# All two-tensor work of GpSimd moved to VectorE, and the gates' last product made a side stream, in a hybrid DeltaNet and pooling block on one core

## The chip, the core and the metric

One core of a Trainium2 chip runs the whole layer. Its engines are TensorE (PE; its weight loads are PEld), VectorE (DVE), ScalarE (ACT), GpSimd (POOL) and SyncE (SP), which issues the transfers. The metric is the device time of one execution in microseconds (us).

## What is computed

One layer of a hybrid block, batch 1: 1024 tokens `x` and 256 context tokens `ctx`, 1024 channels. Normalised and modulated tokens go through one input projection whose columns feed two groups of heads: eight DeltaNet heads (scans in both directions, the tokens' scans starting from the context's final states) and four pooling groups with box means of width 2, 4, 8 and 16. Both are gated by a SiLU, joined, projected, gated, added to `x` and normalised. Cut to what matters:

```python
hn = _rms_norm(h, gain) * (1 + scale) + shift
proj = jnp.einsum('bld,dp->blp', hn, w_in)
qkv, ab, z_dn, u_pool, z_pool = jnp.split(proj, PROJ_SPLITS, axis=-1)
qkv = jax.nn.silu(_short_conv(qkv, conv_w))          # 5 taps
...                                                  # q, k, v per head, l2-normalised
o_f, s_f = _gated_delta_rule(q, k, v, g[0], beta[0], s0_f)
o_b, s_b = _gated_delta_rule(flipped ..., s0_b)
o = _rms_norm(o_f + jnp.flip(o_b, 2), dn_gain) * jax.nn.silu(z_dn)
y_pool = _pool_mixer(u_pool, ...) * jax.nn.silu(z_pool)
y_x = jnp.concatenate([o, y_pool], axis=-1)
out = _rms_norm(x + gate_x * jnp.einsum('blm,md->bld', y_x, w_out), final_gain)
...                                                  # delta rule, a chunk: q_dec = q * exp(g)
v_new = u_i - w_i @ state
o_i = q_dec_i @ state + qk_i @ v_new
state = state * exp(g_last) + k_tail_i^T @ v_new
```

## The kernel before

**Precision.** The input projection is made in a split form. Each weight tile (1024 x 128, `wraw`) is copied to a rounded `whi` on ACT, and the rest, `wlo = wraw - whi`, is made on POOL; the activations have `hnhi` and `hnlo` likewise. Three matmuls per k step (hi by hi, hi by lo, lo by hi) make 24 for a half tile of 512 tokens (rows `mm<-hnhi,whi`, `mm<-hnhi,wlo`, `mm<-hnlo,whi`; in the context's tiles of 256 tokens the sources are called `D` and `zs`). The output projection does the same with `yhi`, `ylo`, `wohi` and `wolo`.

**Stages.** Modulation and the context's tiles (the head of the program, to some 165 us); then for each of the eight heads four projection tiles, v, k, z, q (to 925); then the pooling (to 1110) and the output projection. A head's q, k and v pass a convolution of five taps (`conv_post`): four multiply-adds on VectorE per half, `kT<-u,cw,kT` and its like, a tanh on ACT, and a last product. A gate tile (`gate_tile`: z of the heads, the pooling's u and z) takes a tanh on ACT to `tmp`, and a product on VectorE, `zs<-tmp,mm` or `u<-tmp,mm`.

**The scan.** Beside the projection run side streams: the inverse of each block's triangular matrix (`B`, `bt`, `VV`, `XT`, many small matmuls), the decays `D` (loaded, then masked by selects on POOL), `ks` (scaled keys) and `qd` (queries times their decay, two products of 128x1024 per head on POOL, in `stage_s`), and the scan itself: `sc` and `o` on TensorE, `r` and the state `S` on VectorE. `sm<-sm,expo` on POOL is a power for the norms.

**Order.** The order on each engine is made by a planner while the program is written (class `Flow`). The main stream is the projection, a matmul at a time; a side stream is advanced when its next step is due by the planner's own cost of each instruction (`spend` adds it to the engine). A step that yields a name such as ("conv", i) waits until that flag is set. `conv_tile` waits for the convolution two tiles back, so a k tile waits for the q of the head before: the pause of the main matmuls there is called a seam below. In `spend`, `hold` prices the overlap of POOL's two-tensor work with VectorE's (0 through the heads, 0.9 in the pooling stage).

Of the kernel before, what the change touches and what calls it, by code (L numbers as in the profile page):

```python
# [11 lines left out]
ACTF = mybir.ActivationFunctionType  # L12
ALU = mybir.AluOpType
# [4 lines left out]
P = 128  # L18
# [22 lines left out]
LAG = 6  # L41
T_MOD = 36000.0
T_X = 1500.0
XD = 2
WD = 0
DY = 2
XACT = 9
# [22 lines left out]
class Flow:  # L70
# [3 lines left out]
    def __init__(self):  # L74
        self.free = dict(pe=0.0, act=0.0, dve=0.0, pool=0.0, sync=0.0)
        self.dma = 0.0
        self.cur = None
        self.flags = {}
        self.sides = []
        self.seen = {}, {}  # L80
        self.slots = {}
        self.stored = 0.0
        self.banks = [0.0, 0.0]
        self.port = dict(dve=[], pool=[])

        self.hold = 0.0


    def born(self, name, place, bufs):
# [39 lines left out]
                            del old[r]  # L129
            self.seen[w].setdefault(name, {})[p0, p1, f0, f1, eng] = end  # L130

    def spend(self, eng, ns, uses, shared=False):
        hold = self.hold
        start = self.start(eng, uses)
        end = start + ns
        if shared:

            there = self.port["pool" if eng == "dve" else "dve"]
            both = sum(max(0.0, min(end, b) - max(start, a)) for a, b in there)
            if eng == "dve":  # L140
                end += hold * both
            else:
                self.free["dve"] += hold * both
            self.port[eng] = self.port[eng][-3:] + [(start, end)]
        self.free[eng] = end
        self.note(eng, uses, end)
        t = self.cur
        if t is not None:
            t.next = max(t.next, end + NEXT[eng])
            t.last = eng  # L150
# [177 lines left out]
class Engine:  # L328
# [46 lines left out]
    def __getattr__(self, op):  # L375
        f = getattr(self.real, op)

        def call(*a, **k):
            u = self.uses(op, a, k)
            shared = (op == "tensor_tensor" if self.name == "pool" else  # L380
                      self.name == "dve" and not any(v[0].split("_")[0] in PSUM_TAGS for v in u))
            self.flow.spend(self.name, self.cost(op, a, k), u, shared)
            return f(*a, **k)  # L383

        return call
# [24 lines left out]
def kernel(  # L410
# [235 lines left out]
    def hnc(b, k, t0=0):  # L646
        return (hnc_lo if b else hnc_hi)[k // 4][:, k % 4, :]
# [3 lines left out]
    def ctx_split(k):  # L651
        tp = pp_tile()
        for i, xt in enumerate(cx_t):
            pe.transpose(tp[:, i * P:(i + 1) * P], xt[:, k * P:(k + 1) * P], ident)
        h32 = dl_tile([P, 512], "tmp", 2)
        act.activation(out=h32[:, 0:LC], in_=tp[:, 0:LC], func=ACTF.Identity,
                       scale=md[:, 1, 1, k:k + 1], bias=md[:, 1, 0, k:k + 1])
        dve.tensor_copy(hnc(0, k), h32[:, 0:LC])
        (dve if k % 2 else pool).tensor_tensor(out=hnc(1, k), in0=h32[:, 0:LC], in1=hnc(0, k), op=ALU.subtract)

    def hnx(b, k, t0):
        return hn[2 * (t0 // 512) + b][:, k, :]
# [26 lines left out]
    def split(raw, hi, lo, e):  # L689

        act.activation(out=hi, in_=raw, func=ACTF.Copy)
        e.tensor_tensor(out=lo, in0=raw, in1=hi, op=ALU.subtract)

    def w_split(n, part):
        if n >= len(order):
            return
        if part == 0:
            wq[n] = [gemm.tile([P, KT, P], FP32R, tag=f"w{s}", bufs=2, name=f"w{s}") for s in ("hi", "lo")]
        hi, lo = wq[n]
        s = slice(part * (KT // 2), (part + 1) * (KT // 2))  # L700
        split(raws[n][:, s, :], hi[:, s, :], lo[:, s, :], dve if n < WD and part else pool)

    arrs = [{a: const.tile([P, 16, n], FP32, name=f"{a}{i}") for a in ("ngc", "neg", "edl", "egl", "beta")}
            for i, n in enumerate((NBC, NB))]
# [37 lines left out]
    def gemm_take():  # L742
        i = cur[0]
        cur[0] += 1
        if i + 2 < N2:
            w_load(i + 2)
        return i, wq.pop(i)

    def gemm_half(i, w, src, t0, m, evac):
        ps = mm_tile()  # L750
        j = 0
        for k in range(KT):
            for a, b in PASSES:
                pe.matmul(ps[:, 0:m], w[a][:, k, :], src(b, k, t0),
                          start=(j == 0), stop=(j == 3 * KT - 1))
                j += 1
                if t0 == 0 and j == (4 if i > 1 else 14) and i:
                    w_split(i + 1, 0)
                if t0 == 0 and j == (14 if i > 1 else 18) and i:
                    w_split(i + 1, 1)  # L760
                    if i + 2 >= N2:
                        w_load(i + 2)
                yield
        evac(ps[:, 0:m], t0)

    def gemm_tile(src, n, evac):
        i, w = gemm_take()
        for t0 in range(0, n, 512):
            yield from gemm_half(i, w, src, t0, min(512, n), evac)

# [46 lines left out]
        if name:  # L817
            flow.flag(*name)

    def gate_tile(src, dst, tmp=lambda: dl_tile([P, 512], "tmp", 2)):  # L820
        def evac(ps, t0):
            t = tmp()
            act.activation(out=t, in_=ps, func=ACTF.Tanh, scale=0.5)
            dve.scalar_tensor_tensor(out=dst[:, t0:t0 + 512], in0=t, scalar=1.0, in1=ps,
                                     op0=ALU.add, op1=ALU.mult)

        yield from gemm_tile(src, L, evac)


    ab_src = {}  # L830
# [430 lines left out]
    def stage_s(J):  # L1261

        J.qd = [J.load_rows(escr, d, dl_tile([P, 8 * P], "qd", 2)) for d in range(2)]
        yield from stage_k(J)
        for d in range(2):
            pool.tensor_tensor(out=J.qd[d], in0=J.qd[d], in1=J.qT, op=ALU.mult)
        flow.flag("q", J.key)

    def scan_step(J, blocks, S, Sn, first, last, o, ostart):
# [190 lines left out]

    def z_tile(h):
        zs = dl_tile([P, L], "zs", 2)
        yield from gate_tile(hnx, zs)
        jobs[h].zs = zs
        flow.flag("z", h)

    def zp_tile(t):

        yield ("hn",)
        if t > 1:  # L1470
            yield ("zp", t - 2)
        zs = dl_tile([P, L], "ks", 2)
        yield from gate_tile(hnx, zs)
        sync.dma_start(out=zscr[CH[t]], in_=zs)
        flow.flag("zp", t)

    def zp_late(t):
        i = convs[0]
        yield ("conv", i - 2)
        zs = dl_tile([P, L + 4], "u", 2)  # L1480
        convs[0] += 1
        yield from gate_tile(hnx, zs)
        sync.dma_start(out=zscr[CH[t]], in_=zs[:, 0:L])
        flow.flag("conv", i)

    def u_early(n):

# [126 lines left out]
    for k in range(KT):  # L1614
        if k == PRE:
            for g, n in zip(start, (2, 3, 3)):
                for _ in range(n * KT // 2):
                    next(g)
        mod_part(1, mod_ps[1], k)
        if k < KT // 2:  # L1620
            ctx_split(k)
        if k >= SPOS and k - SPOS < 4:
            w_split((k - SPOS) // 2, (k - SPOS) % 2)
    act.activation(out=alg, in_=alg, func=ACTF.Exp)
    mod_end(1, mod_ps[1])
    for k in range(KT // 2, KT):
# [3 lines left out]
    flow.add(gate_all(), [("k", -1)])  # L1630
    flow.run(main())
    flow.drain()
    flow.hold = 0.9
    dl.release()


# [22 lines left out]
    def icnt_tile(hw):  # L1659
        f = [pl([P, GW], f"ic{i}") for i in range(3)]  # L1660
        r = []
        for n, t in ((GW, f[0]), (GR, f[1])):
            pool.tensor_scalar(out=t[:, 0:n], in0=idf[:, 0:n], scalar1=float(hw), scalar2=float(n),
                               op0=ALU.add, op1=ALU.min)
            pool.tensor_scalar(out=f[2][:, 0:n], in0=idf[:, 0:n], scalar1=float(-hw), scalar2=0.0,
                               op0=ALU.add, op1=ALU.max)
            pool.tensor_tensor(out=t[:, 0:n], in0=t[:, 0:n], in1=f[2][:, 0:n], op=ALU.subtract)
            dve.reciprocal(out=t[:, 0:n], in_=t[:, 0:n])
            r.append(t[:, 0:n])
        ic = pl([P, GR, GW], "icnt", 2)  # L1670
        pool.tensor_tensor(out=ic, in0=rep(r[0], GR), in1=bc(r[1], GW), op=ALU.mult)
        return ic

    def window_ranges(m, n):
# [128 lines left out]
    def u_tiles(between):  # L1803
# [10 lines left out]
        for a in post:  # L1814
            if a == "z":
                t, zs = next(stage)
                yield from gate_tile(hnx, zs, lambda: pl([P, 512], "ws", 3))
                sync.dma_start(out=zscr[t], in_=zs)
                flow.flag("zl", t)
                continue  # L1820
            if n >= NU:
                yield ("up", CH[n - NU])
# [7 lines left out]
            if n < KT - 2:  # L1830
                yield from gemm_tile(hnx, L, evac)
                flow.flag("u", n)
            else:
                last.append((n, *gemm_take(), evac))
                yield from gemm_half(*last[-1][1:3], hnx, 0, 512, evac)
            n += 1
        between()
# [9 lines left out]
    def out_main():  # L1847
# [18 lines left out]
        def load_split(hi, lo, src, eng, name, after=None):  # L1866
# [4 lines left out]
            def thread():  # L1871
# [15 lines left out]
                yield after  # L1887
                if after:
                    yield
                yield eng  # L1890
                h, l = (hi, lo)
                if after:
                    h, l = wo[name[1]] = hi()
                split(r, h, l, dve if eng == "dve" else pool)
                free_raw(slot)
                flow.flag(*name)

# [88 lines left out]

        def second_half():
            yield ("mixed",)
            flow.hold = 0.0
# [113 lines left out]
```

## Time and profile before

| what | value |
|---|---|
| median of 3 runs | 1295.55 us (1290.17 to 1296.2) |
| the profiled execution | 1298.5 us, its span 1296.8 us |
| mean granted TensorE clock | 0.966 |
| busy in the span | PE 1205.6, DVE 906.3, ACT 582.3, POOL 412.7 us |

The times in the rows count from the first instruction of the span. A row of instructions gives how many there were, what they took in all, the mean of one, and behind a second bar how long the engine had been idle just before them and what ended that. L383 is a helper through which each instruction of the kernel before is recorded (L366 in the changed one), so rows are told apart by tile names.

### The profile page before, as it was taken

To read this page: it belongs to the slowest core of one execution; us is meant where nothing else is said; L and a number is where in the kernel's file an instruction comes from. 1 tells how busy PE (TensorE), PEld (TensorE's weight loads), DVE (VectorE), ACT (ScalarE), POOL (GpSimd) and SP (SyncE) were. 2 spreads that over 40 slices of the span, in tenths; PEclk is the share of its full clock that TensorE was granted. 3 is DMA by queue.
4 is the path that set the end of the run, shared out by engine and by line. 5 is a ranking of instruction groups with operands and counts; after the bars stand their busy time and mean duration, and the time that the engine had idled before them with its cause. 6 is when DMAs were issued, how large, how long until landed. Compare 5 with 4: busy or idle time off the path is not lost.

```text
span 1296.8 us, 26417 instructions
## 1 busy us (share of the span) xinstructions
PE 1205.6 (93%) x10631; PEld 968.8 (75%) x10631; DVE 906.3 (70%) x1867; ACT 582.3 (45%) x1514; POOL 412.7 (32%) x447
## 2 busy tenths in 40 slices
PE   7875799999899999999999999999999998989997
PEld 1674677787687877877778778778788886768886
DVE  4798689769785777787887887888434999733212
ACT  2476637543445537555474474653613223222110
POOL 2466433121321423324233142141215643313230
PEclk9898799899898999999999999999999998999999
DMA  9542255222121323112221132122313135574230
GB/s 318 208 114 82 58 144 155 75 58 69 43 62 22 102 50 103 41 43 87 65 86 39 47 102 58 46 80 51 96 58 106 49 122 187 175 251 134 83 113 33
DMA packets 157384, 123.73 MB, mean 95 GB/s; under 512 B 47106, under 2 KB 135115, under 8 KB 157261
## 3 DMA queue, kind: packets, MB, share of 16 engines
q1 hardware_dynamic: 157261, 122.04, 31.3%
q8 instruction: 83, 1.36, 0.4%
q14 instruction: 40, 0.33, 0.1%
HBM read 101.43 MB, written 20.60 MB: 94 GB/s over the span
## 4 chain that ended last, share of the span: by engine, by line
PE 54%; DVE 26%; ACT 8%; DMA 5%; issue 4%; POOL 2%; SPq 0%; DVEq 0%; POOLq 0%; ACTq 0%
PE mm L383 34%; PE sc L383 6%; DVE kT L383 6%; PE o L383 6%; DVE t L383 5%; PE pp L383 5%; PE pa L383 4%; DVE vT L383 3%; ACT junk L383 2%; DVE qT L383 1%; DVE B L383 1%; DVE D L383 1%; ACT u L383 1%; DVE ws L383 1%; ACT ks L383 1%
## 5 line engine op out<-in xcount | busy, mean ns | idle before, releaser
L383 PE MATMUL mm<-hnhi,wlo 128*128 128x512 f32 x768 | 319.0, 415 | 0.0
L383 PE MATMUL mm<-hnhi,whi 128*128 128x512 f32 x768 | 318.7, 415 | 0.0
L383 PE MATMUL mm<-hnlo,whi 128*128 128x512 f32 x768 | 315.7, 411 | 0.0
L383 POOL TENSOR_TENSOR wlo<-wraw,whi 128x512 fp32r<-128x512 f32 x110 | 159.0, 1452 | 389.5 <-ACT whi L383 385.5
L383 PEld LDWEIGHTS mm<-hnhi,wlo 128*128 128x128 f32 x768 | 146.7, 191 | 24.7 <-issue 0.9
L383 PEld LDWEIGHTS mm<-hnhi,whi 128*128 128x128 f32 x768 | 146.8, 191 | 23.8 <-issue 0.9
L383 PEld LDWEIGHTS mm<-hnlo,whi 128*128 128x128 f32 x768 | 146.8, 191 | 22.7
L383 DVE SCALAR_TENSOR_TENSOR kT<-u,cw,kT 128x512 f32<-128x512 f32 (+1 forms) x96 | 99.1, 1035 | 5.4 <-ACT kT L383 1.8
L383 ACT ACTIVATE y<-sc 128x256 f32<-128x256 f32 (+1 forms) x65 | 25.1, 386 | 126.4 <-PE sc L383 121.0
L383 DVE SCALAR_TENSOR_TENSOR t<-t,laneN 128x1 f32<-128x1 f32 (+4 forms) x150 | 62.7, 418 | 13.8 <-POOL t L383 8.2
L383 ACT ACTIVATE u<-mm 128x512 f32<-128x512 f32 (+1 forms) x64 | 34.6, 541 | 80.9 <-PE mm L383 80.9
L383 ACT ACTIVATE whi<-wraw 128x512 fp32r<-128x512 f32 x110 | 67.2, 631 | 2.1 <-DMA wraw<-in_w_in_dram 1.8
L383 DVE SCALAR_TENSOR_TENSOR vT<-u,cw,vT 128x512 f32<-128x512 f32 (+1 forms) x80 | 66.4, 838 | 1.8
L383 DVE TENSOR_TENSOR pw<-mm,zp 128x512 f32<-128x512 f32 (+1 forms) x12 | 8.0, 669 | 81.3 <-PE mm L383 81.3
L383 ACT ACTIVATE D<-D,ngc 128x128 f32<-128x128 f32 x160 | 53.1, 404 | 25.9 <-POOL D L383 25.7
L383 DVE SCALAR_TENSOR_TENSOR qT<-u,cw,qT 128x512 f32<-128x512 f32 (+1 forms) x80 | 61.3, 772 | 3.9 <-ACT qT L383 2.2
L383 DVE SCALAR_TENSOR_TENSOR S<-S,egl,sc 128x128 f32<-128x128 f32 x112 | 33.6, 341 | 35.6 <-PE sc L383 33.1
L383 DVE SCALAR_TENSOR_TENSOR r<-sc,neg,vn 128x128 f32<-128x128 f32 x128 | 38.6, 343 | 16.7 <-PE sc L383 16.7
L383 DVE SCALAR_TENSOR_TENSOR D<-pp,sm,D 128x128 f32<-128x128 f32 x128 | 35.6, 343 | 20.3 <-PE pp L383 20.3
L383 PEld LDWEIGHTS sc<-r,B 128*128 128x128 f32 x256 | 36.1, 190 | 18.1 <-issue 8.2
L383 PE MATMUL sc<-r,B 128*128 128x128 f32 x256 | 40.9, 282 | 9.3 <-DVE r L383 9.3
L383 PE MATMUL sc<-S,kT 128*128 128x128 f32 x256 | 40.8, 282 | 8.8 <-DVE S L383 8.6
(411 smaller groups left out, 2759.8 us busy)
## 6 DMA issues: line engine op xcount, KB each, us to landing
wraw<-in_w_in_dram SPq DMA_DIRECT2D x55, 512.0 KB, 3.9
D<-gscr SPq DMA_DIRECT2D x40, 256.0 KB, 4.0
qd<-escr SPq DMA_DIRECT2D x16, 512.0 KB
kT<-in_w_in_dram SPq DMA_DIRECT2D x9, 512.0 KB, 4.0
whnhi<-in_w_mod_dram SPq DMA_DIRECT2D x8, 512.0 KB, 3.6
whnlo<-in_w_mod_dram SPq DMA_DIRECT2D x8, 512.0 KB, 9.0
D<-in_w_mod_dram SPq DMA_DIRECT2D x8, 512.0 KB, 3.6
yscr<-zs SPq DMA_DIRECT2D x8, 512.0 KB, 2.9
```

Source lines behind the costliest of these rows:

```text
L383: return f(*a, **k)
```

## The change

What POOL did with two tensors goes to VectorE: the weights' low parts, low parts of activations (`XD`, the context's split), the `qd` products, the inverse counts `icnt`, and the low parts of the output projection. POOL keeps the selects, the powers and the memsets. The low part of a weight is now a side stream of its own (`w_low`, put first among the side streams), and `gemm_take` waits for both of its halves. The gate's last product becomes a side stream (`gate_mul`), with the store and the flag behind it, and a half tile waits for the gate product two back. The planner's price of overlap (`hold`, `port`) is gone. In the loading of the output weights the ACT and the VectorE part are separate steps.

```diff
-XD = 2
+XD = 1
...
-    def spend(self, eng, ns, uses, shared=False):
-        hold = self.hold
+    def spend(self, eng, ns, uses):
         start = self.start(eng, uses)
-        end = start + ns
-        if shared:
-
-            there = self.port["pool" if eng == "dve" else "dve"]
-            both = sum(max(0.0, min(end, b) - max(start, a)) for a, b in there)
-            if eng == "dve":
-                end += hold * both
-            else:
-                self.free["dve"] += hold * both
-            self.port[eng] = self.port[eng][-3:] + [(start, end)]
-        self.free[eng] = end
+        end = self.free[eng] = start + ns
...
-        (dve if k % 2 else pool).tensor_tensor(out=hnc(1, k), in0=h32[:, 0:LC], in1=hnc(0, k), op=ALU.subtract)
+        dve.tensor_tensor(out=hnc(1, k), in0=h32[:, 0:LC], in1=hnc(0, k), op=ALU.subtract)
...
-    def w_split(n, part):
+    def w_split(n, part, now=False):
         if n >= len(order):
             return
         if part == 0:
             wq[n] = [gemm.tile([P, KT, P], FP32R, tag=f"w{s}", bufs=2, name=f"w{s}") for s in ("hi", "lo")]
-        hi, lo = wq[n]
-        s = slice(part * (KT // 2), (part + 1) * (KT // 2))
-        split(raws[n][:, s, :], hi[:, s, :], lo[:, s, :], dve if n < WD and part else pool)
+        hi, lo = (t[:, part * (KT // 2):(part + 1) * (KT // 2), :] for t in wq[n])
+        raw = raws[n][:, part * (KT // 2):(part + 1) * (KT // 2), :]
+        act.activation(out=hi, in_=raw, func=ACTF.Copy)
+        flow.flag("whi", n, part)
+        if now:
+            dve.tensor_tensor(out=lo, in0=raw, in1=hi, op=ALU.subtract)
+            flow.flag("wlo", n, part)
+        else:
+            flow.add(w_low(n, part, raw, hi, lo), [("whi", n, part)], True)
+
+    def w_low(n, part, raw, hi, lo):
+        yield "dve"
+        dve.tensor_tensor(out=lo, in0=raw, in1=hi, op=ALU.subtract)
+        flow.flag("wlo", n, part)
+        if part and n + 1 >= N2:
+            w_load(n + 1)
...
     def gemm_take():
         i = cur[0]
         cur[0] += 1
+        for part in range(2):
+            if ("wlo", i, part) not in flow.flags:
+                yield ("wlo", i, part)
         if i + 2 < N2:
             w_load(i + 2)
         return i, wq.pop(i)
 
     def gemm_half(i, w, src, t0, m, evac):
+        if gates[0] and ("gate", gates[0] - 1) not in flow.flags:
+            if ("gate", gates[0] - 2) not in flow.flags and gates[0] > 1:
+                yield ("gate", gates[0] - 2)
...
-                    if i + 2 >= N2:
-                        w_load(i + 2)
...
-        i, w = gemm_take()
+        i, w = yield from gemm_take()
...
+    gates = [0]
+
+    def gate_tile(src, dst, tmp=lambda: dl_tile([P, 512], "tmp", 2), store=None, name=None):
+
         def evac(ps, t0):
+            n = gates[0]
+            gates[0] += 1
             t = tmp()
             act.activation(out=t, in_=ps, func=ACTF.Tanh, scale=0.5)
-            dve.scalar_tensor_tensor(out=dst[:, t0:t0 + 512], in0=t, scalar=1.0, in1=ps,
-                                     op0=ALU.add, op1=ALU.mult)
+            flow.flag("tanh", n)
+            flow.add(gate_mul(n, t, ps, t0, dst, store, name), [("tanh", n)], True)
 
         yield from gemm_tile(src, L, evac)
+
+    def gate_mul(n, t, ps, t0, dst, store, name):
+        yield "dve"
+        dve.scalar_tensor_tensor(out=dst[:, t0:t0 + 512], in0=t, scalar=1.0, in1=ps, op0=ALU.add, op1=ALU.mult)
+        flow.flag("gate", n)
+        if t0:
+            if store is not None:
+                sync.dma_start(out=store, in_=dst[:, 0:L])
+            flow.flag(*name)
...
-            pool.tensor_tensor(out=J.qd[d], in0=J.qd[d], in1=J.qT, op=ALU.mult)
+            yield "dve"
+            dve.tensor_tensor(out=J.qd[d], in0=J.qd[d], in1=J.qT, op=ALU.mult)
...
         zs = dl_tile([P, L], "zs", 2)
-        yield from gate_tile(hnx, zs)
+        yield from gate_tile(hnx, zs, name=("z", h))
         jobs[h].zs = zs
-        flow.flag("z", h)
...
-    flow.hold = 0.9
...
-        pool.tensor_tensor(out=ic, in0=rep(r[0], GR), in1=bc(r[1], GW), op=ALU.mult)
+        dve.tensor_tensor(out=ic, in0=rep(r[0], GR), in1=bc(r[1], GW), op=ALU.mult)
...
-                yield eng
+                yield "act"
                 h, l = (hi, lo)
                 if after:
                     h, l = wo[name[1]] = hi()
-                split(r, h, l, dve if eng == "dve" else pool)
+                act.activation(out=h, in_=r, func=ACTF.Copy)
+                yield
+                yield "dve"
+                dve.tensor_tensor(out=l, in0=r, in1=h, op=ALU.subtract)
```

The planner orders the rest anew. Three places follow.

TensorE, in the head: `mm` are the context's projection tiles, `pp<-ident,...` and `pa` the transposes and products that prepare the blocks of the tokens' scan. Before:

```order
L383 MATMUL mm<-D_220,wlo 128x256
L383 MATMUL pp<-ident,B 128x128 x8
L383 MATMUL pp<-ident,ks 128x128 x2
L383 MATMUL pp<-ident,qd 128x128 x2
L383 MATMUL pa<-kT 128x128 x4
L383 MATMUL pp<-ident,ks 128x128 x2
L383 MATMUL pp<-ident,qd 128x128 x2
L383 MATMUL pp<-kT 128x128 x4
```

and in the changed kernel, where the same step comes some 95 rows sooner:

```order
L366 MATMUL pa<-kT 128x128 x4
L366 MATMUL pp<-ident,ks 128x128 x2
L366 MATMUL pp<-ident,qd 128x128 x2
L366 MATMUL mm<-D_219,whi 128x256
L366 MATMUL mm<-zs,whi 128x256
L366 MATMUL mm<-D_219,wlo 128x256
L366 MATMUL mm<-D_219,whi 128x256
L366 MATMUL mm<-zs,whi 128x256
```

Before, the transposes stand in one piece behind the last of the context's matmuls; now they stand between the context's matmuls, two or three at a time.

VectorE, where a head's k taps run (`kT<-u,cw,kT`). Before:

```order
L383 SCALAR_TENSOR_TENSOR kT<-u,cw,kT 128x512 x4
L383 TENSOR_SCALAR VV<-pp 32x8x32 x2
L383 SCALAR_TENSOR_TENSOR kT<-u,cw,kT 128x512 x4
L383 TENSOR_SCALAR B<-pp 64x8x64
L383 SCALAR_TENSOR_TENSOR zs<-tmp,mm 128x512
L383 SCALAR_TENSOR_TENSOR r<-sc,neg_234,vn 128x128 x2
L383 SCALAR_TENSOR_TENSOR kT<-u,kT 128x512 x2
L383 TENSOR_TENSOR B<-pa,ident 128x512
```

and in the changed kernel:

```order
L366 SCALAR_TENSOR_TENSOR kT<-u,cw,kT 128x512 x2
L366 TENSOR_TENSOR wlo<-wraw,whi 128x512
L366 SCALAR_TENSOR_TENSOR kT<-u,cw,kT 128x512 x2
L366 TENSOR_TENSOR wlo<-wraw,whi 128x512
L366 SCALAR_TENSOR_TENSOR kT<-u,cw,kT 128x512 x4
L366 TENSOR_TENSOR qd<-qd,qT 128x1024 x2
L366 TENSOR_SCALAR B<-pp 64x8x64
L366 SCALAR_TENSOR_TENSOR zs<-tmp,mm 128x512
L366 SCALAR_TENSOR_TENSOR kT<-u,kT 128x512 x2
```

The two weight lows and the pair of `qd` products stand among the taps now, and `r` stands behind the taps' last products.

TensorE, in the seam ahead of head 6's k tile, from the last matmul of the tile before to the first of the k tile. Before:

```order
L383 MATMUL mm<-hnhi_225,wlo 128x512
L383 MATMUL o<-y,D_6622 128x128 x2
L383 MATMUL pa<-laneN,B 32x16 x16
L383 MATMUL sc<-S,kT 128x128 x2
L383 MATMUL pa<-laneN,B 32x16 x16
L383 MATMUL o<-S,qd 128x128 x2
L383 MATMUL pp<-qT,kT 128x128 x4
L383 MATMUL pa<-laneN,bt 32x16 x16
L383 MATMUL sc<-r,B 128x128 x2
L383 MATMUL pa<-laneN,bt 32x16 x16
```

and in the changed kernel:

```order
L366 MATMUL mm<-hnhi_225,wlo 128x512
L366 MATMUL sc<-r,B 128x128 x2
L366 MATMUL pa<-laneN,B 32x16 x16
L366 MATMUL o<-y,D_6581 128x128 x2
L366 MATMUL pa<-laneN,B 32x16 x16
L366 MATMUL pa<-laneN,bt 32x16 x32
L366 MATMUL pa<-t_8420,XT 32x16 x48
L366 MATMUL pp<-qT,kT 128x128 x4
L366 MATMUL pa<-t_8420,XT 32x16 x16
L366 MATMUL pp<-ident,ks 128x128 x4
L366 MATMUL mm<-hnhi_223,whi 128x512
```

The scan's steps are fewer in the seam now; small products `pa<-t,XT` of the inverse and the transposes of `ks` stand in it instead.

## Rows read from the trace of the kernel before

**Rows 1.** The page: busy time, share and instructions of each engine; the chain by engine.
```profile
PE 1205.6 (93%) x10631; PEld 968.8 (75%) x10631; DVE 906.3 (70%) x1867; ACT 582.3 (45%) x1514; POOL 412.7 (32%) x447
...
PE 54%; DVE 26%; ACT 8%; DMA 5%; issue 4%; POOL 2%; SPq 0%; DVEq 0%; POOLq 0%; ACTq 0%
```
**Rows 2.** The span in five windows: length, busy us of each engine, granted clock, DMA.
```profile
0.00:165.00 165.00, 123.72 (x646) 89.48 (x647) 119.78 (x235) 90.47 (x206) 81.23 (x126) 0.86 0.48 156
165.00:500.00 335.00, 320.56 (x3793) 255.92 (x3791) 257.54 (x613) 166.98 (x456) 87.70 (x97) 0.97 0.28 76
500.00:925.00 425.00, 406.50 (x4386) 332.79 (x4386) 338.87 (x796) 230.38 (x675) 121.77 (x124) 1.00 0.23 65
925.00:1110.00 185.00, 179.29 (x1019) 146.75 (x1019) 127.62 (x149) 55.86 (x115) 83.72 (x68) 0.98 0.35 110
1110.00:1297.00 187.00, 175.51 (x795) 143.88 (x793) 62.52 (x77) 38.62 (x63) 38.28 (x32) 0.97 0.41 131
```
**Rows 3.** The same view of one stretch of the head.
```profile
114.60:142.00 27.40, 12.96 (x64) 10.65 (x62) 22.02 (x48) 18.38 (x34) 15.09 (x13) 0.62 0.13 39
```
**Rows 4.** TensorE's waits, 50 to 165: total us, times, longest.
```profile
PE pp L383 <- ACT W L383: 10.7, 2, 9.8
```
**Rows 5.** TensorE's waits, 500 to 925.
```profile
PE sc L383 <- DVE r L383: 9.3, 9, 1.6
PE sc L383 <- DVE S L383: 6.9, 7, 1.6
```
**Rows 6.** Timelines of GpSimd and VectorE from 593: start, us, instruction, count.
```profile
594.99 5.61 POOL L383 TENSOR_TENSOR qd<-qd,qT 128x1024 f32<-128x1024 f32 x2
...
593.07 8.08 DVE L383 SCALAR_TENSOR_TENSOR kT<-u,cw,kT 128x512 f32<-128x512 f32 x4
```
**Rows 7.** Timeline of VectorE at 732.
```profile
732.45 1.54 DVE L383 SCALAR_TENSOR_TENSOR qT<-u,cw,qT 128x512 f32<-128x512 f32 x2
```
**Rows 8.** VectorE's instructions by form: busy us, mean ns | idle before, releaser.
```profile
L383 DVE SCALAR_TENSOR_TENSOR kT<-u,cw,kT 128x512 f32<-128x512 f32 x64 | 77.5, 1215 | 2.6
...
L383 DVE SCALAR_TENSOR_TENSOR qT<-u,cw,qT 128x512 f32<-128x512 f32 x64 | 49.2, 774 | 1.2
...
L383 DVE SCALAR_TENSOR_TENSOR zs<-tmp,mm 128x512 f32<-128x512 f32 x16 | 11.0, 687 | 13.7 <-ACT tmp L383 13.7
...
L383 DVE SCALAR_TENSOR_TENSOR u<-tmp,mm 128x512 f32<-128x512 f32 x12 | 8.2, 686 | 19.9 <-ACT tmp L383 19.9
...
L383 DVE TENSOR_TENSOR hnlo<-XT,hnhi 128x512 fp32r<-128x512 f32 x4 | 2.7, 686 | 2.2 <-ACT hnhi L383 2.2
```
**Rows 9.** GpSimd's instructions by form, whole span.
```profile
L383 POOL TENSOR_TENSOR wlo<-wraw,whi 128x512 fp32r<-128x512 f32 x110 | 159.0, 1452 | 389.5 <-ACT whi L383 385.5 <-issue 3.8
L383 POOL TENSOR_TENSOR qd<-qd,qT 128x1024 f32<-128x1024 f32 x16 | 42.7, 2692 | 0.0
...
L383 POOL TENSOR_TENSOR wlo<-kT,whi 128x512 fp32r<-128x512 f32 x18 | 24.3, 1359 | 9.0 <-ACT whi L383 8.9
```
**Rows 10.** Timeline of VectorE in the pooling stage.
```profile
1008.46 1.23 DVE L383 TENSOR_TENSOR ws<-ws,icnt 128x1024 f32<-128x1024 f32 x1
```
**Rows 11.** VectorE's instructions by form, 50 to 165.
```profile
L383 DVE SCALAR_TENSOR_TENSOR kT<-u,cw,kT 128x256 f32<-128x256 f32 x28 | 19.6, 701 | 2.6 <-ACT kT L383 1.8
L383 DVE SCALAR_TENSOR_TENSOR vT<-u,cw,vT 128x256 f32<-128x256 f32 x16 | 14.8, 925 | 0.5
```
**Rows 12.** Timeline of VectorE at 60.
```profile
60.09 0.48 DVE L383 SCALAR_TENSOR_TENSOR kT<-u,cw,kT 128x256 f32<-128x256 f32 x1
```
**Rows 13.** TensorE's waits, 165 to 500.
```profile
PE o L383 <- DVE qd L383: 3.9, 3, 3.1
```
**Rows 14.** The window view of the seam before head 6's k tile.
```profile
734.10:739.30 5.20, 5.20 (x156) 4.58 (x155) 4.08 (x12) 2.24 (x4) 0.14 (x2) 1.00 0.01 3
```
**Rows 15.** Timelines of ScalarE and GpSimd, 739 to 751.
```profile
740.52 0.28 ACT L383 ACTIVATE junk<-o 128x128 f32<-128x128 f32 x1 [0.68 <-PE o L383]
...
747.84 2.18 ACT L383 ACTIVATE ks<-o,sm 128x128 f32<-128x128 f32 x8
...
745.55 2.26 POOL L383 TENSOR_TENSOR sm<-sm,expo 128x8 f32<-128x8 f32 x1
```

More of the change, by code (lines that the diff above doesn't have):

```diff
@@ L83, in __init__ @@
         self.banks = [0.0, 0.0]
-        self.port = dict(dve=[], pool=[])
-        self.hold = 0.0
     def born(self, name, place, bufs):
@@ L378, in call @@
         def call(*a, **k):
[L379 to L382, printed above, removed]
+            self.flow.spend(self.name, self.cost(op, a, k), self.uses(op, a, k))
             return f(*a, **k)
@@ L818, in conv_post @@
             flow.flag(*name)
-    def gate_tile(src, dst, tmp=lambda: dl_tile([P, 512], "tmp", 2)):
+    gates = [0]
+    def gate_tile(src, dst, tmp=lambda: dl_tile([P, 512], "tmp", 2), store=None, name=None):
         def evac(ps, t0):
+            n = gates[0]
+            gates[0] += 1
             t = tmp()
             act.activation(out=t, in_=ps, func=ACTF.Tanh, scale=0.5)
-            dve.scalar_tensor_tensor(out=dst[:, t0:t0 + 512], in0=t, scalar=1.0, in1=ps,
-                                     op0=ALU.add, op1=ALU.mult)
+            flow.flag("tanh", n)
+            flow.add(gate_mul(n, t, ps, t0, dst, store, name), [("tanh", n)], True)
         yield from gemm_tile(src, L, evac)
+    def gate_mul(n, t, ps, t0, dst, store, name):
[6 more added lines that the diff above has]
+            flow.flag(*name)
     ab_src = {}
@@ L1472, in zp_tile @@
         zs = dl_tile([P, L], "ks", 2)
-        yield from gate_tile(hnx, zs)
-        sync.dma_start(out=zscr[CH[t]], in_=zs)
-        flow.flag("zp", t)
+        yield from gate_tile(hnx, zs, store=zscr[CH[t]], name=("zp", t))
     def zp_late(t):
@@ L1481, in zp_late @@
         convs[0] += 1
-        yield from gate_tile(hnx, zs)
-        sync.dma_start(out=zscr[CH[t]], in_=zs[:, 0:L])
-        flow.flag("conv", i)
+        yield from gate_tile(hnx, zs, store=zscr[CH[t]], name=("conv", i))
     def u_early(n):
@@ L1622 @@
         if k >= SPOS and k - SPOS < 4:
-            w_split((k - SPOS) // 2, (k - SPOS) % 2)
+            w_split((k - SPOS) // 2, (k - SPOS) % 2, True)
     act.activation(out=alg, in_=alg, func=ACTF.Exp)
@@ L1816, in u_tiles @@
                 t, zs = next(stage)
-                yield from gate_tile(hnx, zs, lambda: pl([P, 512], "ws", 3))
-                sync.dma_start(out=zscr[t], in_=zs)
-                flow.flag("zl", t)
+                yield from gate_tile(hnx, zs, lambda: pl([P, 512], "ws", 3), zscr[t], ("zl", t))
                 continue
@@ L1833, in u_tiles @@
             else:
-                last.append((n, *gemm_take(), evac))
+                last.append((n, *(yield from gemm_take()), evac))
                 yield from gemm_half(*last[-1][1:3], hnx, 0, 512, evac)
@@ L1988, in second_half @@
             yield ("mixed",)
-            flow.hold = 0.0
             yield ("pw", GROUPS[-1])
```

## Prediction

> **What bounds the kernel now.** I read the busy shares first, then the chain that ended last, then the span cut into stages, then TensorE's waits in each stage. TensorE (PE) is busy 1205.6 of 1296.8 us, VectorE (DVE) 906.3, GpSimd (POOL) 412.7; the chain runs 54% through PE and 26% through DVE, 2% through POOL [rows 1]. So PE sets the pace and DVE is who it waits for. The stages say where: PE's idle time is 165 - 123.7 = 41 us in the head, 335 - 320.6 = 14 us up to 500, 425 - 406.5 = 18.5 us in the steady heads, 6 us in the pooling stage and 11.5 us in the output projection [rows 2]. PE's work is the same before and after the change (the same matmuls), so the time can only come out of these 91 us, out of the clock, or be added to them.
>
> In the head the largest piece is 114.6 to 142, where PE has 13 us of work in 27.4 at a granted clock of 0.62, which is TensorE's lower level (1.2 GHz) for most of the stretch [rows 3]; one wait of 9.8 us stands in it [rows 4]. The main matmuls of the projection stop there: all that is left of preparing the scan's first blocks stands in the program at that one place. In the steady heads nearly all the named waits are for DVE's `r` and `S`, 9.3 + 6.9 us [rows 5].
>
> **What the change gives DVE back.** While POOL ran a pair of `qd` products (5.61 us), four k taps on DVE took 8.08 us [rows 6]; undisturbed, two taps took 1.54 [rows 7]. So the pair cost DVE 8.08 - 4 x 0.77 = 5.0 us, 0.89 us of DVE for each us of POOL. The means agree: k taps, which lie beside the weights' low parts and `qd`, take 1215 ns, q taps of the same shape 774 [rows 8]. From below, the 64 k taps alone give back 64 x 0.44 = 28 us. From above, POOL's low parts and `qd` in the table (159.0 + 42.7 + 24.3 = 226 us, [rows 9]) times 0.89 would be 201, but much of that lies beside idle DVE or one-input work. A sum over all forms, mean less the shortest instance, gives about 120; I take that.
>
> The Trainium skill ("SBUF — State Buffer", section "Who interferes with whom") states that a DVE instruction with two SBUF inputs and a GpSimd instruction that reads SBUF share a port as an exclusive lock, so that the later one stops until the first is done. The rows of the pair agree nearly fully (0.89 where the lock alone would give at most 1.0, or 5.6 us instead of 5.0). By that rule the selects on `D` that stay on POOL would go on holding DVE up; the sum takes nothing back for these.
>
> **What the change adds to DVE.** 128 low parts of weights (110 + 18 by POOL's rows) at 0.686 us, the time of the same subtraction of that shape on DVE [rows 8]: 88 us. 16 `qd` products of 128x1024 at 1.23 us, an undisturbed product of that shape [rows 10]: 20. Activations' low parts, output lows and inverse counts, some 40 instructions by the same two prices: about 36. Together 144 us. DVE's volume thus goes from 906 to 906 + 144 - 120 = 930 (72%), or, with the lower bound of 28, to 1022 (79%). In volume the change is about neutral; what counts is the place.
>
> **Head.** The order of DVE's instructions before the first `bt<-B` (139.6 us before) holds 30 weight lows, 9 activation lows and 4 context lows more, and 22 taps fewer: 39 x 0.686 + 4 x 0.48 - 22 x 0.48 = 18 us more. Given back: taps of 128x256 take 701 and 925 ns [rows 11] where an undisturbed one takes 0.48 [rows 12]: 28 x 0.22 + 16 x 0.44 = 13 us, with the q taps and tap ends 23, with all two-input forms 33. So DVE comes there 5 to 15 us sooner. PE's stop at 114.6 is a wait for just this work, and in the changed order its transposes stand among the context's matmuls instead of behind them, so PE meets DVE's work without a second bill. A lower bound of nothing isn't excluded: two milestones further on DVE's lead is 7. I take **-11**, above the middle, since the 27.4 us at 0.62 also give clock back.
>
> **165 to 500.** 14 us idle, of which one wait of 3.1 us is for `qd` [rows 13], now made earlier in DVE's own order. The same means speak for a gain: **-3**, bounds 0 and -8.
>
> **500 to 925.** Each head's k taps run into `qd`. Before: 8.08 us for four taps, then `B`, `zs`, `r`. After: 4 x 0.77 + 2 x 1.23 = 5.5, then `B`, `zs`, two more products, `r`: 1.0 us sooner for `r`, and other instructions come 2.6 sooner. I take half of the 16.2 us of `r` and `S` waits: -8, bounds 0 and -16. DVE was at 339 of 425 [rows 2]; new there are 40 lows and 10 `qd`, 27 + 12 = 40 us, and back come 18 (k taps alone) to 37 (all forms): 80 to 85% busy.
>
> Against that stand the seams. A k tile may start only when the convolution of the q two tiles back is finished; before the k tile of head 6 the main matmuls pause from 734.1 to 739.3, 5.2 us, filled with 156 small matmuls [rows 14]. In the changed order three of the eight seams also hold the transposes of `ks`, behind this chain: `o` ready, eight sums of squares on ACT (3.1 us), POOL's power (2.26), four of eight scalings on ACT (1.1) [rows 15]. With the 0.68 us before the first sum and the hops between engines that is some 7.5 us behind the first matmul, a hole of 9 instead of 5.2, of which 2.4 us is PE work that was done elsewhere before: +1.4 each, **+4** for the three. Net **-4**.
>
> **Gates.** The gate's last product stood in the main stream, and DVE waited for ACT's tanh before it, 13.7 + 19.9 us in all [rows 8]. As a side stream it lets other DVE work go first. I cost it at nothing, since DVE isn't the bound in those stretches and PE's next tile covers it (the gate's PSUM bank is asked for two halves later); without that cover a half tile would wait for one product, 0.69 us.
>
> **Pooling and output.** PE idles 6 and 11.5 us there. The lows of `y` and the output weights (13 of 1024 columns and smaller) cost DVE some 30 us where it is 69% busy and 33% busy [rows 2], and about as much contention leaves. **0**, bounds -5 and +6.
>
> **The sum.** -11 - 3 - 4 + 0 = -18. The profiled execution took 1298.5 us (span 1296.8), so 1280.5 on its basis; the median of the runs shown is 1295.55, 3 below, which makes **1278**.
>
> **Rivals.**
> Large gain: the head gives its 15, and the waits between 165 and 925 go almost wholly (25 of 33 us idle), the seams costing nothing. 1295.5 - 40 = 1256. For it: the means of the taps show DVE held up everywhere; against it: DVE isn't emptier, only smoother.
> No change: the head gives 5, the waits halve to no effect since `r` comes only 1.0 us sooner, the seams take 4: 1295.5 - 5 - 3 + 4 = 1291.5, up to 1297. For it: volume is neutral, and four fifths of PE's idle time lie outside the steady heads.
> Slower: the seams decide. If in all eight of them the chain over ACT and POOL ends last and no PE work moves into the hole, each costs 9 - 5.2 = 3.8 us: +30, less the head's 11: 1295.5 + 19 = 1314.5. It decides from three seams' full price (11) upward. What speaks for it is that DVE then has 80 to 85% and every late `qT` makes the next k tile late; against it, that the order shows `ks` in three seams only. The Trainium skill ("Perfetto Trace Analysis", section "Optimizing Scalar/DVE Operations") says that work may be taken off a saturated DVE, to GpSimd even, though the shared port may eat the gain. By its first half this change goes the wrong way, by its second it costs nothing; the row of the pair, 5.0 us of DVE lost for 2.5 us of work moved, bears out the second.
>
> **How the numbers follow.** The forecast has 0.45 (its own range 1266 to 1289), the large gain 0.20, no change 0.19, slower 0.16. Faster, same and slower part at 0.5% of the median, 1289.1 and 1302.0, about what a measurement of this kernel can tell from no change: 0.65, 0.19, 0.16. For 8 in 10 the range must take in most of the large gain and all of no change: 1252 to 1302, leaving out the slower case and 4 in 100 at the low end.
>
> **What would show it.** Right: k taps of 512 columns near 0.77 us; `qd` near 1.23 on DVE; the stretch at 114.6 shorter by about 11 us; `r` and `S` waits near 8 us in the steady heads; DVE near 930 us busy. Wrong: k taps still over 1 us (something else on POOL holds them); seams over 9 us at every k tile; PE waiting for `wlo`, now on DVE behind taps, in the steady heads (each tile's lows are due half a tile ahead, so I expect none); DVE over 1000 us.

## The result, and the profile after

The changed kernel takes 1270.89 us (median of 4 runs, 1267.3 to 1271.24) against 1293.33 before (1290.17 to 1296.2): a ratio of 0.9824, 95% interval 0.9802 to 0.9845, 22 us less. The forecast was 1278, 17.5 less. The profiled execution took 1271.0 us, 27.5 less than the one of before.

The page of the changed kernel, busy times and the chain [rows 1]:

```profile
PE 1199.5 (95%) x10631; PEld 969.3 (76%) x10631; DVE 915.1 (72%) x2050; ACT 579.8 (46%) x1514; POOL 109.0 (9%) x264
...
PE 65%; DVE 14%; issue 8%; ACT 7%; DMA 5%; POOL 0%; SPq 0%; DVEq 0%; POOLq 0%; ACTq 0%
```

GpSimd has lost 304 of its 413 us, and VectorE has gained only 9, with 183 instructions more. What GpSimd keeps is selects, memsets and powers; the powers are products of two tensors too, but small ones (128x8), so the title's "all" goes a little too far. TensorE's idle time fell from 91 to 70 us, its busy time by 6. The instructions of VectorE by form say why its volume stood still [rows 8, 9]:

```profile
L366 DVE TENSOR_TENSOR wlo<-wraw,whi 128x512 fp32r<-128x512 f32 x110 | 75.8, 695 | 11.2 <-ACT whi L366 11.1
L366 DVE SCALAR_TENSOR_TENSOR kT<-u,cw,kT 128x512 f32<-128x512 f32 x64 | 48.2, 760 | 2.0
...
L366 DVE TENSOR_TENSOR qd<-qd,qT 128x1024 f32<-128x1024 f32 x16 | 19.1, 1218 | 0.0
...
L366 DVE SCALAR_TENSOR_TENSOR zs<-tmp,mm 128x512 f32<-128x512 f32 x16 | 11.0, 684 | 2.7 <-ACT tmp L366 2.4
...
L366 DVE SCALAR_TENSOR_TENSOR u<-tmp,mm 128x512 f32<-128x512 f32 x12 | 8.2, 682 | 12.7 <-ACT tmp L366 12.7
```

A k tap takes 760 ns where it took 1215; a weight's low part takes 0.695 us on VectorE where it took 1.45 on GpSimd. Behind the second bar stands the other half: VectorE waited 15 us for the gates' tanh, where it had waited 34.

To compare stages, the windows must end at the same work, not at the same time. The ends chosen are the starts of the projection's main matmuls 480, 1248 and 2208 (counted from 0 in order of time, without those of the modulation) and the last one of the pooling's tiles. Before:

```profile
0.00:181.70 181.70, 140.42 (x964) 99.80 (x965) 131.56 (x254) 96.60 (x220) 87.55 (x131) 0.87 0.50 157
181.70:509.60 327.90, 313.45 (x3549) 253.26 (x3548) 253.43 (x605) 168.84 (x466) 83.55 (x94) 0.97 0.26 71
509.60:934.80 425.20, 406.70 (x4498) 332.36 (x4498) 333.14 (x789) 227.01 (x664) 120.87 (x124) 1.00 0.24 68
934.80:1084.50 149.70, 149.48 (x761) 124.44 (x759) 100.70 (x127) 41.80 (x92) 64.32 (x61) 1.00 0.31 98
1084.50:1296.80 212.30, 195.52 (x866) 158.95 (x864) 87.50 (x95) 48.05 (x74) 56.42 (x39) 0.96 0.42 133
```

and in the changed kernel:

```profile
0.00:160.30 160.30, 135.76 (x963) 94.73 (x964) 123.40 (x308) 97.95 (x226) 21.33 (x81) 0.89 0.57 179
160.30:482.80 322.50, 312.06 (x3622) 252.63 (x3621) 261.99 (x641) 171.49 (x478) 28.95 (x62) 0.98 0.27 76
482.80:915.50 432.70, 412.84 (x4461) 342.03 (x4461) 334.29 (x836) 223.20 (x658) 36.97 (x70) 0.96 0.22 64
915.50:1062.90 147.40, 147.07 (x725) 123.07 (x724) 106.02 (x163) 40.08 (x82) 15.80 (x35) 1.00 0.33 103
1062.90:1269.30 206.40, 191.77 (x867) 156.84 (x865) 89.41 (x105) 47.11 (x71) 5.99 (x16) 0.97 0.42 134
```

The head gained 21.4 us, the first heads 5.4, the pooling 2.3, the output 5.9; the steady heads lost 7.5, and their granted clock fell from 1.00 to 0.96. Of these 7.5 us TensorE is idle for 1.4 more (18.5 before, 19.9 now) and busy for 6.1 more, with 37 matmuls fewer in the stage. The lower clock comes in four stretches of 34 us in all, where the granted clock is 0.50, the lower level (1.2 GHz); three begin inside one of the last seams, while TensorE stands or does small matmuls, and one 4 us behind the seam at 532. In the kernel before no stretch of the steady heads is at that level. One of the four:

```profile
794.10:804.30 10.20, 7.92 (x148) 6.94 (x149) 8.28 (x19) 8.57 (x25) 2.22 (x3) 0.50 0.01 3
```

The stop of the main matmuls [rows 3] is gone: in 106 to 124, where the transposes stand now, TensorE is busy 17.3 of 18 us at full clock.

```profile
106.00:124.00 18.00, 17.31 (x99) 14.60 (x99) 17.55 (x41) 14.19 (x37) 1.27 (x2) 1.00 0.44 119
```

In the steady heads the waits for `r` and `S` [rows 5] have nearly gone, and another has come. TensorE's waits, 500 to 925:

```profile
PE pa L366 <- ACT t L366: 11.5, 4, 3.6
...
PE sc L366 <- DVE r L366: 1.3, 1, 1.3
```

Three of the four, 3.3 to 3.6 us long, stand in the last three seams. Timelines of TensorE and ScalarE at the seam ahead of head 6's k tile [rows 14, 15]:

```profile
709.99 1.48 PE L366 MATMUL pa<-t,XT 32*32 32x16 f32 x96 [3.56 <-ACT t L366]
...
705.54 0.28 ACT L366 ACTIVATE junk<-o 128x128 f32<-128x128 f32 x1 [0.80 <-PE o L366]
...
708.62 1.05 ACT L366 ACTIVATE u<-qT 128x1024 f32<-128x1024 f32 x1
709.56 0.37 ACT L366 ACTIVATE t<-pa 128x256 f32<-128x256 f32 x1
```

ScalarE does the eight sums of squares, then the q tanh, and only then the copy `t` that TensorE needs. The last main matmul before this seam and the first after it start 11.9 us apart, against 5.2 before.

### The profile page after: what moved, and what is told of

Read it like the earlier page. It is cut to its first block, busy times and chain, and to the rows that moved or that the text cites. A ratio compares the mean times of both kernels' runs of the same rounds, so it can differ in the third digit from the quotient of the medians.

```text
span 1269.3 us, 26407 instructions
## 1 busy us (share of the span) xinstructions
PE 1199.5 (95%) x10631; PEld 969.3 (76%) x10631; DVE 915.1 (72%) x2050; ACT 579.8 (46%) x1514; POOL 109.0 (9%) x264
## 4 chain that ended last, share of the span: by engine, by line
PE 65%; DVE 14%; issue 8%; ACT 7%; DMA 5%; POOL 0%; SPq 0%; DVEq 0%; POOLq 0%; ACTq 0%
PE mm L366 42%; PE pp L366 8%; PE o L366 5%; PE sc L366 5%; DVE t L366 4%; PE pa L366 4%; DVE qT L366 2%; ACT junk L366 2%; DVE wlo L366 2%; DMA wraw<-in_w_out_dram 1%; DVE kT L366 1%; DVE vT L366 1%; DVE S L366 1%; ACT u L366 1%; DMA whnlo<-in_w_mod_dram 1%
## 5 line engine op out<-in xcount | busy, mean ns | idle before, releaser
L366 DVE TENSOR_TENSOR wlo<-wraw,whi 128x512 fp32r<-128x512 f32 x110 | 75.8, 695 | 11.2 <-ACT whi L366 11.1
L366 DVE SCALAR_TENSOR_TENSOR kT<-u,cw,kT 128x512 f32<-128x512 f32 (+1 forms) x96 | 64.3, 674 | 3.0 <-ACT kT L366 0.4
L366 DVE SCALAR_TENSOR_TENSOR vT<-u,cw,vT 128x512 f32<-128x512 f32 (+1 forms) x80 | 56.2, 707 | 1.3
L366 DVE SCALAR_TENSOR_TENSOR qT<-u,cw,qT 128x512 f32<-128x512 f32 (+1 forms) x80 | 54.9, 692 | 1.3
L366 DVE SCALAR_TENSOR_TENSOR t<-t,laneN 128x1 f32<-128x1 f32 (+4 forms) x150 | 48.0, 320 | 5.2 <-DMA laneN<-ds 1.4
L366 ACT ACTIVATE ks<-pp,sm 128x128 f32<-128x128 f32 x160 | 43.7, 399 | 2.7 <-PE pp L366 2.7
L366 PEld LDWEIGHTS sc<-S,kT 128*128 128x128 f32 x256 | 36.5, 190 | 10.4 <-issue 4.9
L366 POOL TENSOR_TENSOR sm<-sm,expo 128x8 f32<-128x8 f32 x18 | 30.9, 1714 | 155.0 <-DVE sm L366 154.2
L366 PE MATMUL mm<-D,wlo 128*128 128x256 f32 x128 | 38.6, 301 | 5.2 <-DVE wlo L366 5.1
```

## The experiments

All times are medians against the kernel before, run in the same set (its medians: 1293.4 for 1 to 4, 1294.7 for 5 to 8, 1293.4 for 9 to 12). Where stages are named, they end at the same main matmuls as above.

**1 and 2. Order and engine apart.** Each kernel keeps one order and swaps the engine that the moved work is issued on; the planner still counts it for the other. In the changed kernel (in the one before it is the same with `nc.vector` and "pool"):

```diff
+    alt = Engine(flow, nc.gpsimd, "dve")
-        dve.tensor_tensor(out=lo, in0=raw, in1=hi, op=ALU.subtract)
+        alt.tensor_tensor(out=lo, in0=raw, in1=hi, op=ALU.subtract)
...
```

> The changed kernel's program, step for step in the changed kernel's order, but every piece of work that the change moved (weights' low parts, half of the activations' low parts, decayed queries, inverse counts, low parts of the output projection) is issued on GpSimd again. Theory 1 (the engine: VectorE is no longer held up while GpSimd works on two tensors) expects the gain to go: k taps at about 1.2 us again and 1285 to 1305 us. Theory 2 (the order: the planner's new order, above all the head where the transposes stand among the context's matmuls, brings the gain) expects 1268 to 1278.

> The kernel before, step for step in its own order, but the moved work is issued on VectorE where GpSimd stood; gates and waits as before. Theory 1 (the engine) expects most of the gain without any new order: 1270 to 1280 us, with k taps near 0.76 us and the stretch at 114.6 shorter by 10 to 15. Theory 2 (the order) expects 1288 to 1298, and VectorE's weight lows queued ahead of what TensorE waits for could even make it slower.

Measured: new order on GpSimd 1321.0 us (ratio 1.0214, 1.0170 to 1.0257); old order on VectorE 1326.7 (1.0262, 1.0231 to 1.0292). Both theories fell (the second had named a slower kernel as possible, without a number): either half alone is slower than before by 28 to 33 us, and only the two together are faster. In the first, VectorE's k taps are slow again:

```profile
L366 DVE SCALAR_TENSOR_TENSOR kT<-u,cw,kT 128x512 f32<-128x512 f32 x64 | 81.1, 1275 | 2.6
```

Even so main matmul 480 starts 10.4 us sooner than before; the loss stands in all the stages behind it. In the second the taps take 780 ns, and main matmul 480 starts 8.9 us sooner; all this is lost behind it, 15.5 us up to main matmul 1248 and 26.1 in the steady heads. VectorE's waits there:

```profile
DVE wlo L383 <- ACT whi L383: 66.8, 39, 4.6
```

A low part stands in VectorE's line where it stood in GpSimd's, right behind its high part. GpSimd could stand and wait for ScalarE (394 us in the kernel before [rows 9]; TensorE waited 3.8 us for those low parts); when VectorE stands and waits, `r`, `S` and the taps stand behind it. In the steady heads TensorE's idle time is 36.8 us instead of 18.5, and most of its waits are for VectorE:

```profile
PE sc L383 <- DVE S L383: 12.1, 15, 1.6
PE o L383 <- DVE qd L383: 8.7, 10, 1.1
```

**3. The gates' last product back in the main stream.**

```diff
-            flow.add(gate_mul(n, t, ps, t0, dst, store, name), [("tanh", n)], True)
+            for _ in gate_mul(n, t, ps, t0, dst, store, name):
+                pass
```

> The changed kernel with one part undone: the gate's last product is issued in the main stream right behind its tanh again, the planner orders the rest. The forecast costed the gates' side stream at nothing: 1268 to 1275 us. The rival, that the 33.6 us which VectorE waited for the tanh were worth something, expects 1278 to 1290.

Measured: 1295.8 (1.0035, 1.0005 to 1.0064): 25 us more than the changed kernel, the rival's case and beyond. VectorE's waits:

```profile
DVE wlo L366 <- ACT whi L366: 23.9, 21, 2.6
DVE zs L366 <- ACT tmp L366: 21.8, 12, 3.5
DVE u L366 <- ACT tmp L366: 21.3, 12, 6.0
```

43 us for the tanh, where the changed kernel has 15; the waits for high parts grow too, from 11 to 24. The loss stands in the first heads (11 us against the changed kernel), the steady heads (10) and the pooling (5). How it reaches TensorE isn't taken apart: its idle time over the whole span grows by 10.5 us, its busy time by 17, and the order is another one too.

**4. The convolution of q first.**

```diff
-        flow.add(conv_post(u, n, ct, dst, name, i), [("evac", i)])
+        flow.add(conv_post(u, n, ct, dst, name, i), [("evac", i)], n == L and ct < H)
```

> The changed kernel with one word more: the convolution of a q tile is put first among the side streams. In the order no seam ahead of a k tile then holds 100 small matmuls or more, where the changed kernel has six with 108 to 150. If the holes of 11 to 12 us at the four last seams and the lower clock behind them cost what the stages show (500 to 925 took about 7 us longer than before, and waits of 11.5 us stand there), this gives 1245 to 1262 us. If the holes are only the place where work is done that must be done anyway, it stays at 1266 to 1276.

Measured: 1309.9 (1.0139, 1.0105 to 1.0172), a clear miss. The seams are short, as the order said, but `qd` comes late: TensorE's waits, 500 to 950:

```profile
PE o L366 <- DVE qd L366: 13.8, 10, 2.1
PE sc L366 <- ACT y L366: 9.4, 4, 2.6
```

A hole of 4.2 us with 4 small matmuls in it now stands in each head, and the granted clock of the steady heads is 0.96 here too. That is not the whole loss: against the changed kernel the first heads take 14 us more, the steady heads 7, and the pooling 18, as 956 matmuls fall into that stage instead of 725.

**5 to 7. The parts, planned for.** Here the planner knows the engine and orders anew. 5 keeps both side streams and puts the moved work back on GpSimd; 6 moves the work without side streams; 7 has the gates' side stream alone (the loading of the next weights goes back to its old place with it).

```diff
-        yield "dve"
-        dve.tensor_tensor(out=lo, in0=raw, in1=hi, op=ALU.subtract)
+        yield "pool"
+        pool.tensor_tensor(out=lo, in0=raw, in1=hi, op=ALU.subtract)
...
-        split(raws[n][:, s, :], hi[:, s, :], lo[:, s, :], dve if n < WD and part else pool)
+        split(raws[n][:, s, :], hi[:, s, :], lo[:, s, :], dve)
...
-    def w_split(n, part, now=False):
+    def w_split(n, part, now=True):
```

> The changed kernel with the moved work planned for and issued on GpSimd, as before the change; the side streams (weights' low parts, gates' last product) and the planner without a price of overlap stay. If the side streams need the move and the move needs them, this gives little: 1283 to 1300 us, with k taps at 1.2 us. If the gates' side stream alone is worth the 25 us that its undoing cost, it gives 1265 to 1278.

> The kernel before with the moved work planned for and issued on VectorE, but with no side streams: a weight's low part stands in the program right behind its high part, a gate's product right behind its tanh. The theory that VectorE then stands waiting at the head of its own line (66.8 us for weights' high parts were seen when the old order was run with the work on VectorE) expects 1290 to 1325 us, with 40 to 70 us of such waits. The rival, that the loss came from an order planned for the other engine, expects the planner to mend it: 1272 to 1285.

> The changed kernel with the weights' low parts issued right behind their high parts again, on VectorE; the gates' side stream stays. The theory of waits at the head of VectorE's line expects 1280 to 1305 us with 40 to 60 us of waits for high parts. If the low parts' side stream is worth nothing it stays at 1268 to 1275.

Measured: 5 took 1310.4 (1.0134, 1.0094 to 1.0173), slower than either case expected; by main matmul 480 it is level with the kernel before, then it loses 10 us up to main matmul 1248 and 4 in the steady heads. The pooling's tiles end 19 us later in their stage, but the output stage is 16 shorter, so only 3 are lost there. The planner's price of overlap is gone in 5 too; what that alone costs no run shows. 6 took 1329.8 (1.0289, 1.0243 to 1.0334) and 7 took 1312.4 (1.0148, 1.0114 to 1.0182), both 5 to 7 us beyond their ranges, with longer waits than expected. VectorE's waits in 6 and in 7:

```profile
DVE wlo L383 <- ACT whi L383: 73.6, 52, 4.7
DVE u L383 <- ACT tmp L383: 21.5, 8, 6.0
DVE zs L383 <- ACT tmp L383: 8.4, 5, 2.5
```

```profile
DVE wlo L366 <- ACT whi L366: 84.1, 47, 4.8
```

and in the changed kernel:

```profile
DVE u L366 <- ACT tmp L366: 12.7, 7, 4.4
DVE wlo L366 <- ACT whi L366: 11.1, 7, 2.7
```

The planner doesn't mend it, since without a side stream the low part is issued with the high part and has no later place to go. With 3 this gives a square: the move alone +35 us; with the weights' side stream +2; with the gates' -22 instead of +2, or +18 instead of +35 where the weights' is missing. So the weights' side stream is worth 33 to 40 us, the gates' 17 to 24, each with the order that the planner makes of it. The time doesn't simply follow the waits: 7 waits longer for high parts than 6 and is 17 us faster. With both side streams there, the move itself is worth 38 us (+16 in 5, -22 in the changed kernel).

**8 and 10. The seam.** The sums of squares wait until the q tanh is placed.

```diff
         sm = J.sm
+        if J.h < H - 1:
+            yield ("qin", J.h + 1)
         for b in range(NB):
```

> The changed kernel with one wait more for the planner: the eight sums of squares of a head's output, which stand on ScalarE ahead of the q tanh in the last seams, are placed behind that tanh. In the order one of the four last seams falls from 140 rows to 104 and two below 100. If those sums are what makes the seam's wait of 3.6 us and the lower clock behind it, 1255 to 1266 us; if the work in the hole is due anyway, or the later sums hold up the transposes of the scaled output, 1268 to 1285.

> The changed kernel as it is, beside the others of this set: 1267 to 1274 us.

> The kernel with the sums of squares behind the q tanh once more, in more rounds. Its profiled execution was 1264 with seams of 5.7 to 9.4 us where the changed kernel has 12, two others 1274. If the shorter seams are worth something it lies 2 to 8 us below the changed kernel of this set; if not, within 2.

Measured: 8 took 1270.4 (0.9819, 0.9771 to 0.9867). 10, the same kernel beside the changed one (9), took 1271.3 (0.9825, 0.9790 to 0.9859), and 9 took 1270.4 (0.9827, 0.9790 to 0.9865). The last three seams shrink from 12 to 9.4, 6.6 and 5.8 us, and TensorE's waits for `t` from 11.5 to 4.9 (10):

```profile
PE pa L366 <- ACT t L366: 4.9, 4, 2.6
PE sc L366 <- ACT y L366: 4.6, 3, 2.4
```

The time doesn't move. The small matmuls taken out of the hole (276 in each of the last three seams, now 208, 124 and 148) are done between main matmuls instead, the waits for `y` grow, and the steady heads take 427 and 428 us in place of 431 to 433, less than the runs differ.

**11 and 12. Which of the moved work.** The changed kernel in its own order, with one kind of work on GpSimd.

```diff
-            dve.tensor_tensor(out=J.qd[d], in0=J.qd[d], in1=J.qT, op=ALU.mult)
+            alt.tensor_tensor(out=J.qd[d], in0=J.qd[d], in1=J.qT, op=ALU.mult)
```

> The changed kernel, step for step in its order, with only the 16 products of the decayed queries issued on GpSimd (43 us of GpSimd's work). The theory that the new order on the old engine costs its 50 us in proportion to GpSimd's busy time (226 us of low parts and queries) expects 8 to 12 us more than the changed kernel: 1278 to 1284. The theory that it is only queues and waits around the weights' low parts expects 1268 to 1275.

> The changed kernel, step for step in its order, with only the weights' 128 low parts issued on GpSimd (183 us of GpSimd's work). In proportion to busy time 35 to 42 us more than the changed kernel: 1303 to 1314, with k taps between 0.76 and 1.2 us; if the lows' longer 1.4 us land in time and only contention on taps beside the queries matters, 1278 to 1290.

Measured: queries 1280.9 (0.9905, 0.9868 to 0.9941), 10.5 us more than the changed kernel of the set, as expected; weights' lows 1294.3 (1.0011, 0.9983 to 1.0038), 24 more, between the two cases. If the parts of 1's 50 us add up, some 16 are left for the activations', the outputs' and the inverse counts. The k taps with the queries on GpSimd, and with the lows there:

```profile
L366 DVE SCALAR_TENSOR_TENSOR kT<-u,cw,kT 128x512 f32<-128x512 f32 x64 | 59.5, 936 | 2.0
```

```profile
L366 DVE SCALAR_TENSOR_TENSOR kT<-u,cw,kT 128x512 f32<-128x512 f32 x64 | 57.9, 914 | 2.6
```

Per us of GpSimd's work the queries cost 10.5 / 41 = 0.26 us of the time, the lows 24 / 177 = 0.14. The taps alone don't explain either price. With the lows on GpSimd the steady heads take 432 us, as in the changed kernel (431 in 9), slow taps or not; the head loses 8, the first heads 10 and the stages behind 9. With the queries there the steady heads lose 7 and the first heads 2.5, and a wait stands in them that the changed kernel doesn't have: TensorE waits 7.3 us in all, four times, for the load of a head's state `S`. Two of these waits:

```profile
PE sc L366 <- DMA S<-sscr: 3.6, 2, 3.1
```

## Why the prediction was right, and where it was not

**Sizes of the operations: right.** K taps 0.760 (forecast 0.77), `qd` 1.218 (1.23), weights' lows 0.695 (0.686), VectorE's volume 915 (930). The moved work adds 143 us on VectorE (144), so contention gave back 906 + 143 - 915 = 134 us, where 120 were taken. Experiments 1, 11 and 12 show the cause with the order held: the taps go back to 0.91 to 1.28 us when the work goes back. One reading was off: the four taps of 8.08 us [rows 6] don't all lie beside the pair of `qd` products. The first lies mostly beside a weight's low part (1.46 us), the second half beside a select and half beside the pair (1.00), and only the last two beside the pair alone:

```profile
L383 DVE SCALAR_TENSOR_TENSOR kT<-u,cw,kT 128x512 f32<-128x512 f32 x2 | 5.4, 2724 | 0.1
```

So the pair cost 5.45 - 1.54 = 3.9 us, at most 4.2 with the second tap's share: 0.70 to 0.74 us for each us of GpSimd and not 0.89. The sum doesn't hang on it; the upper bound of 201 us does.

**Head: right place, half the size.** -21.4 instead of -11. The term was worked out for the engine alone, and experiment 2, the engine alone, gave -8.9 up to main matmul 480. Experiment 1, the new order alone, gave -10.4; added up, the two make -19 of the -21. 6 and 7, with the work planned for VectorE and the lows inline, stand at -16 and -17 there.

**165 to 500: right,** -5.4 within bounds 0 and -8.

**500 to 925: wrong sign.** -4 was forecast, +7.5 came. The waits for `r` and `S` went from 16.2 to less than 2 us, more than taken. Against it stand the seams, 11 to 12 us at four of them, not 9 at three. The chain was also another: the wait is for the copy `t` behind the sums of squares and the tanh on ScalarE, not for `ks`. That the holes as such cost the 7.5 us is not borne out: 8 and 10 shortened three of them and the time stayed. What is left is the granted clock, 0.96 against 1.00, with 6.1 of the 7.5 us in busy time. Half of the 34 us at the lower level, 17, is the most that it can be worth. But only some 26 main matmuls fall into these stretches; they start 0.43 us apart instead of 0.23, which makes about 5 us, and the rest of each stretch is waits and small matmuls in the seam. So the clock can explain most of the loss, but that stays open, since no run had the same order at the full clock; 8 and 10 had 0.97 and were 3 to 6 us shorter there.

**Gates: the step that failed.** "I cost it at nothing, since DVE isn't the bound in those stretches" was wrong by 17 to 24 us. VectorE is busy 77% of the steady heads and not the bound, but its order is fixed when the program is written: when it waits 3.5 us for a tanh (3), what is placed behind that product waits too. And no term at all was given to the weights' side stream, which decides the sign: moved without it, the same work makes the kernel 18 us slower (7), and 35 without either side stream (6). The forecast took it, without saying why, that the moved work would cost its duration and no wait, which holds only with the side streams. That the sum came near is in part luck: on the profiled executions -27.5 came for -18, as the head gave 10 us more than taken, pooling and output 8 and the first heads 2 more, and the steady heads 11.5 less.

**Pooling and output:** 0 forecast, -2.3 and -5.9 came, together 3 beyond the lower bound of -5. The output's part comes with the engine: 2 has -6.0 there too. The pooling's was not taken apart.

**The rivals.** "Slower" was priced at seams; its real form is the wait for high parts, which experiments 2, 6 and 7 show and which the change itself avoids. The rule of the Trainium skill ("Perfetto Trace Analysis", section "Optimizing Scalar/DVE Operations") that the shared port may eat the gain of offloading to GpSimd agrees with the volumes here: 304 us taken from GpSimd cost VectorE 9. The rule of the Trainium skill ("SBUF — State Buffer", section "Who interferes with whom") that a VectorE instruction with two SBUF inputs contends with a GpSimd instruction that reads SBUF agrees with the taps, and with the selects that stayed on GpSimd. These hardly show in the means (k taps 760 ns beside q taps of 745), because they lie beside 4 of the changed kernel's 192 taps only. Those four took 0.96 to 1.12 us, where the 173 beside nothing took 0.75 in the mean. Two of them are the first two of these three, which took 2.95 us instead of 2.24:

```profile
223.47 2.77 POOL L366 TENSOR_SCALAR_AFFINE_SELECT D<-D 128x512 f32<-128x512 f32 x2 [6.54 <-DMA D<-gscr]
...
224.63 2.95 DVE L366 SCALAR_TENSOR_TENSOR kT<-u,cw,kT 128x512 f32<-128x512 f32 x3
```

The powers on 128x8 have two inputs as well, and there the measurement shows no hold: taps that lie wholly within a power of 2.1 us took 0.75 us.

## What to carry to other kernels

Before work is moved from an idle engine to a busy one, ask not only what it takes there but what it will wait for there: on GpSimd 394 us of waiting cost TensorE 3.8 us of waits, on VectorE 74 us instead of 24 went with 34 us more (6 against 3). A step that waits for another engine's result should be placed when that result is due, not where it is written. Two changes that are each a loss can together be a gain, so an experiment that undoes one part measures that part only in the company of the others.

## What was not expected of the hardware

The same program comes out in two lengths of the head: in 134 to 165 the granted clock was 0.67 in the first profile of the changed kernel and 0.78 in the second, and main matmul 480 started at 160.4 and at 157.7 us. The runs of one kernel spread by 3 to 16 us, so that gains of a few us, such as that of the seams, can't be told here.
